# Group norms by two products with a tile of ones and the root on all partitions, and state renewals on more ticks, in a hybrid decoder step

## Chip, cores and metric

The kernel runs on one core of a Trainium2 chip. The metric is device time in microseconds (us) of one execution, as the median of several; smaller is better. The core has five engines that run their own instruction streams and meet by semaphores: TensorE (PE, its weight loads PEld), VectorE (DVE), ScalarE (ACT), GpSimd (POOL) and SyncE (SP, which here only issues DMAs).

## What is computed

One layer of a hybrid decoder for 256 new prompt tokens and 64 sample tokens (8 sequences of 8), so 320 tokens with a model width of 2048. One input projection feeds two groups of heads: a gated chunk MLP and a state-space mixer (SSD, Mamba-2). Their outputs go through `w_out`, then comes a feed-forward block with a short convolution. All values are float32. Cut to what the change touches:

```python
def rms_norm(x, w):
    y = x * rsqrt(mean(x * x, axis=-1, keepdims=True) + EPS)
    return y * w

def ssd_mixer(z, xbc, dt_raw, ssm_state, ...):
    ...                                   # convolution, silu, dt
    y, new_state = ssd_scan(xs, dt, a, bm, cm, ssm_state)
    y = (y + d_skip[:, None] * xs).reshape(bsz, L, SSM_WIDTH) * silu(z)
    # the group norm: 4 groups of 512 of the 2048 columns, each with its own mean square
    yg = y.reshape(bsz, L, SSM_GROUPS, SSM_WIDTH // SSM_GROUPS)
    yg = yg * rsqrt(mean(yg * yg, axis=-1, keepdims=True) + EPS)
    y = yg.reshape(bsz, L, SSM_WIDTH) * norm_w
    return y, new_state, new_conv

def decoder_layer(x, ...):
    h = rms_norm(x, norm_mix_pre)
    proj = h @ w_in
    mix = concatenate([gate_out, ssm_out]) @ w_out
    x = x + rms_norm(mix, norm_mix_post)
    f, new_ffn_conv = conv_ffn(rms_norm(x, norm_ffn_pre), ...)
    x = x + rms_norm(f, norm_ffn_post)
```

The states of the 8 sample sequences (each 32 heads x 64 x 128) are outputs too: the old state times its whole decay, plus a product of the 8 new tokens' columns B and of their decayed inputs.

## The kernel before

**Layout.** Activations lie transposed: 128 columns of the model on the partitions, the 320 tokens along the free dimension. A product with weights takes a block of 128x128 weights as the stationary operand and 320 tokens as the moving one.

**Products in parts.** Float32 is computed in three products of a rounded type (`F32R`): both operands are split in a high part, rounded to that type, and a low part, the rest. `accumulate` (L143 to L145) issues high weights by high input, high by low and low by high. `slab` fetches 128x1024 weights by a DMA on SP (tile `wraw`), makes the high part `whi` on ACT (L130) and the low part `wlo` on DVE (L132); each of the three has three buffers. `split` (L367) does the same for activations.

**Passes.** `project` runs one pass over 512 columns of a weight matrix (8 slabs of 24 products), `chunk_out` adds 512 rows of an output matrix into an accumulator (8 slabs of 24 products, evacuated by ACT or DVE, L234 and L236).

**Background tasks and ticks.** What is not a pass is written as generators in a list `bg`. After each slab a pass calls `tick()` `rate` times, and each call advances the first task in the list to its next `yield`; `repeat(None, n)` lets n ticks go by. So the tick decides after which slab a step is written down. Within each engine the instructions are then ordered by a scheduler at build time: by order of writing, unless `first()` or `high_priority` gives a block precedence, and never ahead of what it depends on. `issue_after(x)` keeps an instruction behind x on its engine. What stands in that order is executed in that order.

**The group norm.** `heads_out(g, rate, later)` is called for the four groups g. Its pass makes z; for each block of 128 columns it multiplies y by silu(z), squares it on ACT and adds the squares into `ssq` on DVE (L302), so `ssq` holds for each token 128 partial sums, one a partition. Then the task `norm` is put at the head of `bg`, to run during the next passes: after `later[0]` ticks `token_sums` (L284) lets PE sum `ssq` over the partitions, as three products with a column of ones in float32, which gives the tokens' sums along the partitions (128x3); `rsqrt_of` (L245) takes the reciprocal root of these three columns on DVE, a first guess by integer arithmetic and three Newton steps, eleven operations with precedence; after `later[1]` more ticks `spread` (L288, products L292) brings the result to all partitions and 320 columns by three transposes on PE, and four multiplications (L960), each with a `split` by the norm's weight, make the input of the chunk of `w_out`. `later` is (3, 2) for all groups but the third, where it is (4, 3). The ticks a slab are 1 in the pass behind the first and second norm, 3 behind the third (the pass of the fourth group's z) and 2 behind the fourth (a chunk of `w_out`). `rsqrt_of` has one more user, the layer norm of the gate, on three columns.

**The renewals.** The task `renewals` runs in the feed-forward part, where each of ten rounds of an up-projection and a down-chunk has 24 ticks, and must be finished before the eleventh chunk. It ends three prompt states (`rest`, two ticks each), loads the decays and the first four sample states, then the tokens' columns (`tokens`, 16 DMAs on SP into `xb`). For each of four groups it lets 3 ticks go by, copies the columns (L1191, ACT), masks the low half (L1194, DVE), and for both halves multiplies four states by their decay on POOL (L1199, a tick each), loads the next states, waits two ticks, issues four products of 32 rows on PE (`up_ps`, L1211), adds them to the states on DVE (L1213, a tick each) and stores the states (L1215, from ACT).

**Buffers that matter.** The tag `pv` of the pool `tp` has four buffers of 128x320; the z passes use it for `ev`. PSUM is halved: four banks `mm` for passes and chunks, four banks `ms` (`misc`) for the rest.

Of the kernel before, what the change touches and what calls it, by code (L numbers as in the profile page):

```python
# [9 lines left out]
F32 = mybir.dt.float32  # L10
F32R = mybir.dt.float32r
# [6 lines left out]
P = 128  # L18
# [3 lines left out]
NT = NP + NS  # L22
# [12 lines left out]
def hybrid_step(  # L35
# [10 lines left out]
    act, dve, pool, pe, sp = nc.scalar, nc.vector, nc.gpsimd, nc.tensor, nc.sync  # L46
# [3 lines left out]
    cp = ctx.enter_context(tc.tile_pool(name="cp", bufs=1))  # L50
    dr = ctx.enter_context(tc.tile_pool(name="dr", bufs=1, space=DRAM))
    wp = ctx.enter_context(tc.tile_pool(name="wp", bufs=3))
    tp = ctx.enter_context(tc.tile_pool(name="tp", bufs=2))
# [3 lines left out]
    def misc(name):  # L57
        return ms.tile([P, 512], F32, tag="ms", name=name)
# [6 lines left out]
    with tc.high_priority(offset=300000):  # L65
        dve.memset(ones, 1.0)

        ps = misc("early")
        for _ in range(EARLY):
            pe.matmul(ps[:, :P], ones, ones, start=True, stop=True)  # L70
    upper = cp.tile([P, P], F32, name="upper")
    later = cp.tile([P, P], F32, name="later")
    bd2 = cp.tile([P, P], F32, name="bd2")
# [3 lines left out]
    bd = bd2[:NS, :NS]  # L77

    def masks():
        make_upper_triangular(nc, upper, 1.0, diag=True)  # L80
        make_lower_triangular(nc, later, 1.0, diag=False)
        pool.memset(bd2, 0.0)
        for op, fill, base in ((ALU.is_gt, 1.0, 1 - TS), (ALU.is_ge, 0.0, 0)):
            pool.affine_select(out=bd2, in_=bd2, pattern=[[-TS, P // TS], [0, TS]], compare_op=op, fill=fill, base=base,
                               channel_multiplier=1)

        d4 = ident.rearrange("p (i r t) -> p i r t", r=4, t=TS)
        dve.tensor_reduce(out=low[:, 0:1], in_=d4[:, :, 2:4], axis=mybir.AxisListType.XYZ, op=ALU.add)
        d5 = ident.rearrange("p (i k t) -> p i k t", k=2, t=TS)
        dve.tensor_reduce(out=low[:, 1:2], in_=d5[:, :, 1], axis=mybir.AxisListType.XY, op=ALU.add)  # L90
        dve.tensor_scalar(out=low, in0=low, scalar1=-1.0, scalar2=None, op0=ALU.mult)
        for r in range(2):
            rs = slice(64 * r, 64 * r + 64)
            dve.tensor_tensor(out=upper_s[rs], in0=upper[rs, rs], in1=bd2[rs, rs], op=ALU.mult)
        pool.memset(cmask, 1.0)
        cm4 = cmask.rearrange("p (h b) i -> p h b i", h=2)
        pool.affine_select(out=cm4, in_=cm4, pattern=[[0, 2], [-8, 4], [1, 32]],
                           compare_op=ALU.is_ge, fill=0.0, base=0, channel_multiplier=0)
        pool.affine_select(out=cm4, in_=cm4, pattern=[[0, 2], [8, 4], [-1, 32]],
                           compare_op=ALU.is_ge, fill=0.0, base=7, channel_multiplier=0)  # L100
# [8 lines left out]
    def first():  # L109

        return tc.high_priority(offset=200000)
# [130 lines left out]
        pd_last.append(made)  # L242


    def rsqrt_of(ss, scale, n, rows=P):  # L245

        v = tp.tile([P, n], F32, tag=f"rs_v{n}", name="rs_v")[:rows]
        r = tp.tile([P, n], F32, tag=f"rs_r{n}", name="rs_r", bufs=3)[:rows]
        t = tp.tile([P, n], F32, tag=f"rs_t{n}", name="rs_t")[:rows]
        dve.tensor_scalar(out=v, in0=ss, scalar1=scale, scalar2=EPS, op0=ALU.mult, op1=ALU.add)  # L250
        dve.tensor_scalar(out=r.bitcast(I32), in0=v.bitcast(I32), scalar1=-0.5, scalar2=float(0x5F3759DF),
                          op0=ALU.mult, op1=ALU.add)
        for _ in range(3):
            dve.scalar_tensor_tensor(out=t, in0=v, scalar=-0.5, in1=r, op0=ALU.mult, op1=ALU.mult)
            dve.tensor_tensor(out=t, in0=t, in1=r, op=ALU.mult)
            ins = dve.scalar_tensor_tensor(out=r, in0=t, scalar=1.5, in1=r, op0=ALU.add, op1=ALU.mult).ins
        rsqrt_ins.append(ins)
        return r
# [20 lines left out]
    def token_sums(sq, ps=None, more=False):  # L279

        begins = ps is None
        ps = misc("tsum") if begins else ps
        for c, o in enumerate((0, P, NT - P)):
            ins = pe.matmul(ps[:, c:c + 1], sq[:, o:o + P], ones[:, 0:1], start=begins and c == 0, stop=not more and c == 2).ins  # L284
        sums_ins.append(ins)
        return ps if more else ps[:, 0:3]

    def spread(r, out=None):  # L288

        ps = misc("spread")  # L290
        for c, o in ((2, NT - P), (0, 0), (1, P)):
            spread_ins.append(pe.transpose(ps[:, o:o + P], r[:, c:c + 1].to_broadcast([P, P]), ident).ins)  # L292
        if out is not None:
            act.copy(out, ps[:, :NT])
        return ps[:, :NT]
# [94 lines left out]
    with ExitStack() as mctx:  # L390
# [350 lines left out]
        with tc.tile_pool(name="sd", bufs=1) as sd:  # L741
# [6 lines left out]
            for c in range(3):  # L748
                ps = misc("bt_ps")
# [184 lines left out]
            def heads_out(g, rate, later):  # L934

                ssq = hp.tile([P, NT], F32, tag="ssq", name="ssq")
                y = x_of.pop(g)

                def z_evac(j, ps):
                    if j == 0:  # L940
                        finish(tasks[g])
                    zs = tp.tile([P, NT], F32, tag="ev", name="zs", bufs=2)
                    with first():
                        scaled(ps, AF.Silu, zs)
                        dve.tensor_tensor(out=y[:, j, :], in0=y[:, j, :], in1=zs, op=ALU.mult)
                        add_square(ssq, y[:, j, :], j == 0, dve)
                project(w_in, Z0 + 512 * g, z_evac, quiet=4, rate=rate)

                def norm():
                    yield from repeat(None, later[0])  # L950
                    with tc.issue_after(newest[0]):
                        sums = token_sums(ssq)
                    with first():
                        r = rsqrt_of(sums, 1.0 / 512, 3)
                    yield from repeat(None, later[1])
                    rb = spread(r)

                    res[g] += [h[:, KD - 4:] for h in hT] if g == 3 else out_parts(hp, "o")
                    for j in range(4):
                        dve.tensor_tensor(out=y[:, j, :], in0=y[:, j, :], in1=rb, op=ALU.mult)  # L960
                        split(res[g][0][:, j, :], res[g][1][:, j, :], y[:, j, :], col(prm_at["norm"][3] + 4 * g + j))
                task = norm()
                bg.insert(0, task)
                return task
# [98 lines left out]
    with tc.tile_pool(name="fp", bufs=1) as fp:  # L1063
# [91 lines left out]
        def renewals():  # L1155
# [4 lines left out]
            for g, s1, x1d, _ in rest:  # L1160
                yield from repeat(None, 2)
                with tc.issue_after(rsqrt_ins[-1]):
                    dve.tensor_tensor(out=s1, in0=s1, in1=x1d, op=ALU.add)
                act.dma_start(o_ssm_p[g], s1)

            def load(g, h):

# [19 lines left out]
                tokens(0)  # L1187
            for g in range(4):
                h0 = 8 * g
                yield from repeat(None, 3)  # L1190
                act.copy(part, raw)  # L1191
                yield
                for at, m in ((slice(0, 512), 0), (slice(512, 640), 1)):
                    dve.scalar_tensor_tensor(out=part[:, :, at], in0=part[:, :, at].bitcast(F32), scalar=low[:, m:m + 1], in1=raw[:, :, at],  # L1194
                                             op0=ALU.mult, op1=ALU.add)
                for h in range(2):
                    st = ahead.pop(0)
                    for i in range(4):
                        pool.tensor_tensor(out=by_head(st[i]), in0=by_head(st[i]),  # L1199
                                           in1=tote[:, h0:h0 + 8, 4 * h + i:4 * h + i + 1].to_broadcast([P, 8, 64]), op=ALU.mult)  # L1200
                        yield
                    if h == 0:
                        ahead.append(load(g, 1))
                    elif g < 3:
                        ahead.append(load(g + 1, 0))
                        tokens(g + 1)
                    yield from repeat(None, 2)
                    grown = [misc("up_ps") for _ in range(4)]
                    for i in range(4):
                        at = slice(32 * i, 32 * i + 32)  # L1210
                        pe.matmul(grown[i], part[at, h, 512:], part[at, h, :512], start=True, stop=True, tile_position=(32 * i, 0))  # L1211
                    for i in range(4):
                        dve.tensor_tensor(out=st[i], in0=st[i], in1=grown[i], op=ALU.add)  # L1213
                        yield
                        act.dma_start(o_ssm_s[4 * h + i, g], st[i])  # L1215
# [179 lines left out]
```

## Time and profile before

| | |
|---|---|
| median of 3 runs | 1760.93 us (1760.37 to 1761.53) |
| the profiled execution's own time | 1762.04 us |
| its span in the profile | 1760.3 us |
| busy: PE, PEld, DVE, ACT, POOL | 1751.6, 1729.8, 1154.1, 806.6, 272.7 us |
| instructions on PE | 12178 products and as many weight loads |
| granted PE clock | 0.999 of full speed |
| DMA | 301.38 MB, 171 GB/s in the mean |

The span is shorter than the execution's own time by what lies before its first and behind its last instruction. Rows of a timeline give start (us from the span's start), duration (us), engine, line, operation, tiles (out<-in), shapes and count; a bracket at the end gives the engine's idle time before it and what ended it. Rows of groups give count, then busy us and mean ns of one, then idle time before them and what ended it. A matmul's duration in the profile contains its way through the array, so what a product costs PE in a stream is read from the distance between starts. A float32 product on PE stands as two instructions.

### The profile page before, as it was taken

What the parts mean: (1) busy time and instruction counts of PE and PEld (TensorE: products, weight loads), DVE (VectorE), ACT (ScalarE), POOL (GpSimd) and SP (SyncE); (2) the same over time, 40 slices, a digit from 0 to 9 for tenths busy, and PEclk for the clock granted to TensorE, in tenths of its full rate; (3) what the DMA queues carried; (4) which work ended last, traced back from release to release, by engine and by line L of the source; (5) the groups of instructions that cost most, each with busy time, mean ns of one, the idle gap of its engine ahead of it and who ended that gap; (6) DMA issues with size and microseconds to landing.
All of it is one profiled execution on the core that took longest, in us unless ns stands there. A gap on an engine that the chain in (4) does not pass through costs nothing.

```text
span 1760.3 us, 31124 instructions
## 1 busy us (share of the span) xinstructions
PE 1751.6 (100%) x12178; PEld 1729.8 (98%) x12178; DVE 1154.1 (66%) x1949; ACT 806.6 (46%) x1172; POOL 272.7 (15%) x588
## 2 busy tenths in 40 slices
PE   9999999999999999999999999999999999999998
PEld 9999999999999999999999999999999999999997
DVE  7449754656767576668966677676657565656575
ACT  7344545333854445545544434343434343333335
POOL 1003200000111101021331212130201010111004
PEclk9999999999999999999999999999999999999999
DMA  7466655456665644554756666756454545454542
GB/s 248 144 167 182 185 151 150 153 155 190 216 206 163 201 145 131 166 161 143 228 169 223 189 217 195 222 185 192 151 153 148 156 148 155 148 155 147 155 151 104
DMA packets 228179, 301.38 MB, mean 171 GB/s; under 512 B 19936, under 2 KB 150848, under 8 KB 227840
## 3 DMA queue, kind: packets, MB, share of 16 engines
q1 hardware_dynamic: 215856, 281.27, 52.4%
q10 hardware_dynamic: 10640, 13.60, 2.2%
q0 software_dynamic: 1536, 4.52, 1.0%
q8 instruction: 96, 1.57, 0.4%
q14 instruction: 51, 0.42, 0.1%
HBM read 283.47 MB, written 15.61 MB: 170 GB/s over the span
## 4 chain that ended last, share of the span: by engine, by line
PE 95%; DVE 2%; DMA 1%; ACT 0%; POOL 0%; issue 0%; SPq 0%; POOLq 0%; DVEq 0%; ACTq 0%
PE ps L143 20%; PE ps L145 20%; PE ps L144 20%; PE pd L143 10%; PE pd L144 10%; PE pd L145 10%; PE y_ps L900 1%; DMA wraw<-in_ffn_w_up 1%; DVE wlo L132 1%; PE yo_ps L848 0%; PE sg L705 0%; PE tsum L284 0%; DVE h_lo L374 0%; DVE acc_mix L1042 0%; DMA vt<-in_xT 0%; ACT whi L130 0%
## 5 line engine op out<-in xcount | busy, mean ns | idle before, releaser
L132 DVE TENSOR_TENSOR wlo<-wraw,whi 128x1024 fp32r<-128x1024 f32 x470 | 582.9, 1241 | 436.9 <-ACT whi L130 434.9
L130 ACT CAST whi<-wraw 128x1024 fp32r<-128x1024 f32 x470 | 492.0, 1047 | 730.3 <-PE ps L144 437.7
L143 PE MATMUL ps<-h_hi,whi 128*128 128x320 f32 x2528 | 782.1, 310 | 0.4 <-ACT whi L130 0.4
L144 PE MATMUL ps<-h_lo,whi 128*128 128x320 f32 x2528 | 779.8, 309 | 0.0
L145 PE MATMUL ps<-h_hi,wlo 128*128 128x320 f32 x2528 | 777.8, 309 | 0.0
L143 PEld LDWEIGHTS ps<-h_hi,whi 128*128 128x128 f32 x2528 | 474.8, 188 | 4.2 <-issue 2.3
L144 PEld LDWEIGHTS ps<-h_lo,whi 128*128 128x128 f32 x2528 | 475.1, 188 | 0.0
L145 PEld LDWEIGHTS ps<-h_hi,wlo 128*128 128x128 f32 x2528 | 474.4, 188 | 0.1
L143 PE MATMUL pd<-fhi,whi 128*128 128x320 f32 x704 | 217.2, 309 | 0.0
L144 PE MATMUL pd<-flo,whi 128*128 128x320 f32 x704 | 217.0, 308 | 0.0
L145 PE MATMUL pd<-fhi,wlo 128*128 128x320 f32 x704 | 216.9, 308 | 0.0
L143 PE MATMUL pd<-ohi,whi 128*128 128x320 f32 x448 | 139.5, 312 | 0.0
L145 PE MATMUL pd<-ohi,wlo 128*128 128x320 f32 x448 | 138.5, 309 | 0.0
L144 PE MATMUL pd<-olo,whi 128*128 128x320 f32 x448 | 138.5, 309 | 0.0
L143 PEld LDWEIGHTS pd<-fhi,whi 128*128 128x128 f32 x704 | 132.2, 188 | 0.7 <-issue 0.7
L144 PEld LDWEIGHTS pd<-flo,whi 128*128 128x128 f32 x704 | 132.2, 188 | 0.2 <-issue 0.2
L145 PEld LDWEIGHTS pd<-fhi,wlo 128*128 128x128 f32 x704 | 132.2, 188 | 0.0
L1099 POOL COPY ptf<-pad 128x2 f32<-128x2 f32 x88 | 24.2, 275 | 508.3 <-DVE pad L1087 507.5
L236 DVE TENSOR_TENSOR acc_ffn<-acc_ffn,pd 128x320 f32<-128x320 f32 x160 | 77.2, 482 | 34.5 <-PE pd L145 33.6
L143 PEld LDWEIGHTS pd<-ohi,whi 128*128 128x128 f32 x448 | 84.0, 188 | 1.4 <-issue 0.7
L144 PEld LDWEIGHTS pd<-olo,whi 128*128 128x128 f32 x448 | 84.1, 188 | 0.2 <-issue 0.2
L145 PEld LDWEIGHTS pd<-ohi,wlo 128*128 128x128 f32 x448 | 84.1, 188 | 0.0
(301 smaller groups left out, 1513.6 us busy)
## 6 DMA issues: line engine op xcount, KB each, us to landing
wraw<-in_ffn_w_up SPq DMA_DIRECT2D x176, 512.0 KB
wraw<-in_w_in SPq DMA_DIRECT2D x142, 512.0 KB
wraw<-in_ffn_w_down SPq DMA_DIRECT2D x88, 512.0 KB
wraw<-in_w_out SPq DMA_DIRECT2D x64, 512.0 KB
st<-in_state_ssm SPq DMA_DIRECT2D x64, 256.0 KB
out_ssm_state_sample<-st ACTq DMA_DIRECT2D x32, 256.0 KB
cs<-dacs_d SPq DMA_DIRECT2D x16, 320.0 KB
xr<-in_xT SPq DMA_DIRECT2D x4, 640.0 KB
```

The costliest lines, as they stand in the source:

```text
L130: act.copy(hi[:, :m], raw[:, :m])
L132: dve.tensor_tensor(out=lo[:, :m], in0=raw[:, :m], in1=hi[:, :m].bitcast(F32), op=ALU.subtract)
L143: pe.matmul(ps, whi, xhi, start=first, stop=False)
L144: pe.matmul(ps, whi, xlo, start=False, stop=False)
L145: newest[0] = pe.matmul(ps, wlo, xhi, start=False, stop=last).ins
L236: dve.tensor_tensor(out=acc[:, nb, :], in0=acc[:, nb, :], in1=ps[:, :NT], op=ALU.add)
L900: pe.matmul(ps[64 * i:64 * i + 64, cols], w(hl), x(hl, m, cpx), tile_position=(0, 64 * i), **flags)
L1099: pool.tensor_copy(ptf[:, k, :], pad[:, 256:258])
```

## The change

Four edits. (1) A second tile of ones in the rounded type, `ones_r`, is made from `ones` by a copy on DVE among the masks. (2) In `norm`, the squares are split into a high and a low part (ACT and DVE, with precedence), two ticks sooner than the sums were asked for; one tick behind that, two products of `ones_r` (128x128) with the parts (128x320) give the sums of all tokens on all partitions. The eleven operations of the root then run on 128x320, with `rb` and two buffers of `pv` for its places, and there are no transposes: the four multiplications read `rb`. They are written at the same tick as before, since `later[1] + 1` ticks follow. (3) `rsqrt_of` takes its places from the caller if given. (4) In `renewals`, four ticks follow the prompt states, the first group lets 12 ticks go by in place of 3, and each multiplication on POOL takes two ticks in place of one.

```diff
     def masks():
+        dve.tensor_copy(ones_r, ones)
         make_upper_triangular(nc, upper, 1.0, diag=True)
...
-    def rsqrt_of(ss, scale, n, rows=P):
+    def rsqrt_of(ss, scale, n, rows=P, places=None):
 
-        v = tp.tile([P, n], F32, tag=f"rs_v{n}", name="rs_v")[:rows]
-        r = tp.tile([P, n], F32, tag=f"rs_r{n}", name="rs_r", bufs=3)[:rows]
-        t = tp.tile([P, n], F32, tag=f"rs_t{n}", name="rs_t")[:rows]
+        v, r, t = places or (tp.tile([P, n], F32, tag=f"rs_{name}{n}", name=f"rs_{name}", bufs=bufs)[:rows]
+                             for name, bufs in (("v", 2), ("r", 3), ("t", 2)))
...
                 def norm():
-                    yield from repeat(None, later[0])
+                    yield from repeat(None, later[0] - 2)
+                    parts = [tp.tile([P, NT], F32R, tag="pv", name="ssq_part", bufs=4) for i in range(2)]
+                    with first():
+                        split(*parts, ssq)
+                    yield
+                    ps = misc("tsum")
                     with tc.issue_after(newest[0]):
-                        sums = token_sums(ssq)
+                        for i in range(2):
+                            pe.matmul(ps[:, :NT], ones_r, parts[i], start=i == 0, stop=i == 1)
                     with first():
-                        r = rsqrt_of(sums, 1.0 / 512, 3)
-                    yield from repeat(None, later[1])
-                    rb = spread(r)
+                        rb = sd.tile([P, NT], F32, tag="rb", name="rb", bufs=1)
+                        v, t = (tp.tile([P, NT], F32, tag="pv", name=f"rs_{n}", bufs=4) for n in "vt")
+                        rsqrt_of(ps[:, :NT], 1.0 / 512, NT, places=(v, rb, t))
+                    yield from repeat(None, later[1] + 1)
...
                 act.dma_start(o_ssm_p[g], s1)
+            yield from repeat(None, 4)
...
             for g in range(4):
                 h0 = 8 * g
-                yield from repeat(None, 3)
+                yield from repeat(None, 3 if g else 12)
                 act.copy(part, raw)
...
                                            in1=tote[:, h0:h0 + 8, 4 * h + i:4 * h + i + 1].to_broadcast([P, 8, 64]), op=ALU.mult)
+                        yield
                         yield
```

More of the change, by code (lines that the diff above doesn't have):

```diff
@@ L70, in hybrid_step @@
             pe.matmul(ps[:, :P], ones, ones, start=True, stop=True)
+    ones_r = cp.tile([P, P], F32R, name="ones_r")
     upper = cp.tile([P, P], F32, name="upper")
```

## Prediction

> **What bounds the kernel now.** I read the page first: busy times, then the chain that ended last.
>
> ```profile
> span 1760.3 us, 31124 instructions
> ...
> PE 1751.6 (100%) x12178; PEld 1729.8 (98%) x12178; DVE 1154.1 (66%) x1949; ACT 806.6 (46%) x1172; POOL 272.7 (15%) x588
> ...
> PE 95%; DVE 2%; DMA 1%; ACT 0%; POOL 0%; issue 0%; SPq 0%; POOLq 0%; DVEq 0%; ACTq 0%
> ```
>
> TensorE (PE) is busy all the time and is 95% of the chain; VectorE (DVE) has a third of the span free. A busy PE need not be at its peak, so I looked next at the distances between matmuls, in the timeline of PE around the first group norm:
>
> ```profile
> 529.83 0.31 PE L144 MATMUL ps<-h_lo,whi 128*128 128x320 f32 x1
> ...
> 536.57 0.31 PE L145 MATMUL ps<-h_hi,wlo 128*128 128x320 f32 x1
> 536.72 0.72 PE L284 MATMUL tsum<-ones,ssq 128*128 128x1 f32 x6
> 537.30 0.39 PE L143 MATMUL ps<-h_hi,whi 128*128 128x320 f32 x1
> 537.53 0.31 PE L144 MATMUL ps<-h_lo,whi 128*128 128x320 f32 x1
> ...
> 544.28 0.31 PE L145 MATMUL ps<-h_hi,wlo 128*128 128x320 f32 x1
> 544.42 0.49 PE L292 MATMUL spread<-ident,rs_r 128*128 128x128 f32 x3
> 544.67 0.40 PE L143 MATMUL ps<-h_hi,whi 128*128 128x320 f32 x1
> 544.90 0.31 PE L144 MATMUL ps<-h_lo,whi 128*128 128x320 f32 x1
> ```
>
> The first two rows are 46 steps and 6.74 us apart: one product every 147 ns, without a hole. So time can be won in one way only: issue less on PE, or remove one of its rare waits. Work on other engines is free until PE waits for it. 0.2% of the time, 3.5 us, is about what a measurement of this kernel can tell from no change; the question is whether the change takes more than that off PE.
>
> **The norms: what goes.** From the product before the sums to the second one behind them it is 537.53 - 536.57 = 0.96 us, where two steps take 0.29: the sums cost 0.67. The transposes cost 544.90 - 544.28 - 0.29 = 0.33. I measure to the second product because the first one behind an f32 product holds up the next (537.30 to 537.53 is 0.23, not 0.15). A norm costs 1.00 us of PE, and the tile view counts four of them, six sum products each; in the last one PE also waited before its transposes:
>
> ```profile
> L284 PE MATMUL tsum<-ones,ssq x24: 165/250/250, 536.7 to 751.0; 128*128 128x1 f32 x24
> ...
> 755.32 0.31 PE L144 MATMUL pd<-olo,whi 128*128 128x320 f32 x1
> 755.64 0.51 PE L292 MATMUL spread<-ident,rs_r 128*128 128x128 f32 x3
> ...
> 756.14 0.30 PE L143 MATMUL pd<-ohi,whi 128*128 128x320 f32 x1
> ```
>
> 756.14 - 755.32 - 0.29 = 0.53, so 0.20 more than elsewhere. Removed in all: 4 x 1.00 + 0.20 = 4.2 us.
>
> **The norms: what comes.** Two products of 128x320 with both operands in the rounded type, as the main products have, so at their 147 ns, without the late product behind: 4 x 2 x 0.147 = 1.2 us. The trace has no product with this weight tile; the bounds are 0.29 (the main step) and 0.67 (the sums now) a norm, and I take the first, since shape and type are the main product's. By the Trainium skill, page "TensorE: Matmul & The Clock Gate", section "Back-to-back issue gap", an isolated gap is N/2.4 + 2.5 ns, 136 ns for 320 columns; here the trace shows 147, and by the page's figure the sum would be lower by 0.1 us.
>
> **The norms: what moves to the other engines.** The two parts of the squares cost a copy on ScalarE (ACT) and a subtraction on DVE per norm, and the root runs on 320 columns instead of 3: the same eleven operations. The groups by line give the price of one:
>
> ```profile
> L302 DVE TENSOR_TENSOR ssq<-ssq,sq 128x320 f32<-128x320 f32 x12 | 5.8, 486 | 1.9 <-ACT sq L301 1.8
> L371 DVE TENSOR_TENSOR olo<-s,ohi 128x320 fp32r<-128x320 f32 x16 | 7.7, 484 | 0.6 <-ACT ohi L370 0.5
> L255 DVE TENSOR_TENSOR rs_t<-rs_t,rs_r 128x3 f32<-128x3 f32 x15 | 2.4, 160 | 0.4
> ```
>
> 0.49 us each where it was 0.16. The narrow root's place in DVE's timeline, with what lies around it:
>
> ```profile
> 526.44 0.49 DVE L302 TENSOR_TENSOR ssq<-ssq,sq 128x320 f32<-128x320 f32 x1 [0.60 <-ACT sq L301]
> ...
> 537.48 0.16 DVE L250 TENSOR_SCALAR rs_v<-tsum 128x3 f32<-128x3 f32 x1 [1.88 <-PE tsum L284]
> 537.67 0.17 DVE L251 TENSOR_SCALAR rs_r<-rs_v 128x3 int32<-128x3 int32 x1
> ...
> 538.35 1.22 DVE L132 TENSOR_TENSOR wlo<-wraw,whi 128x1024 fp32r<-128x1024 f32 x1
> ...
> 540.47 0.16 DVE L256 SCALAR_TENSOR_TENSOR rs_r<-rs_t,rs_r 128x3 f32<-128x3 f32 x1
> ...
> 544.95 0.89 DVE L960 TENSOR_TENSOR xs<-xs,spread 128x320 f32<-128x320 f32 x2 [1.68 <-PE spread L292]
> ```
>
> Operations start 0.16 + 0.03 us apart (537.48 to 537.67), so the wide chain takes about 11 x 0.52 = 5.7 us instead of 2.1. The squares are final at 526.9. The parts are asked for two ticks sooner than the sums are now and the products one tick sooner, at the first and second norm about 533 instead of 536.7 (a tick is a slab, 24 steps or 3.5 us). The chain then ends near 534 + 5.7 + 1.2 for one slab's subtraction inside it = 541, and the four multiplications by the root, at 544.95 now because they wait for the transposes, can start 3 to 4 us sooner. At the third and fourth norm, where more ticks fall on a slab, the products stay in their place and the multiplications come some 3 us later than now. In these rows of DVE and PE stand their first (third norm), the first product that uses them, their last (fourth norm) and again the first product:
>
> ```profile
> 726.10 0.88 DVE L960 TENSOR_TENSOR xs<-xs,spread 128x320 f32<-128x320 f32 x2 [0.80 <-PE spread L292]
> 743.50 0.31 PE L143 MATMUL pd<-ohi,whi 128*128 128x320 f32 x1
> 762.24 0.48 DVE L960 TENSOR_TENSOR xs<-xs,spread 128x320 f32<-128x320 f32 x1
> 772.86 0.31 PE L143 MATMUL pd<-h_hi,whi 128*128 128x320 f32 x1
> ```
>
> 17 and 10 us of room; 3 us later costs nothing. What hides the added 3.6 + 0.5 us of DVE per norm is its idle time:
>
> ```profile
> 525.00:553.00 28.00, 28.00 (x195) 27.99 (x195) 16.99 (x38) 11.50 (x15) 1.56 (x6) 1.00 0.50 154
> ```
>
> (PE, PEld, DVE, ACT, POOL, clock.) 28 - 17 = 11 us are free. Queued behind the chain on DVE are the subtractions that make a slab's low part. How late may one be?
>
> ```profile
> 536.77 1.05 ACT L130 CAST whi<-wraw 128x1024 fp32r<-128x1024 f32 x1 [2.43 <-PE ps L144]
> ```
>
> ACT rounds a slab as soon as PE frees one of three buffers, two slabs before the product that needs it: 7.0 - 1.05 - 1.22 = 4.7 us of cover. A chain cut up by subtractions, as now at 538.35, stays inside it; cost nothing. If the cover is gone, each us over it is a us of PE.
>
> Without the transposes the multiplications no longer come late for the output chunks of the first two norms. The weight loads of these chunks waited for them:
>
> ```profile
> L143 PEld LDWEIGHTS pd<-ohi,whi 128*128 128x128 f32 x448 | 84.0, 188 | 1.4 <-issue 0.7 <-ACT s L832 0.4 <-ACT ohi L373 0.3
> ```
>
> 0.3 us for ACT's part of the result. I count it as won (bounds 0 and 0.3).
>
> The cast of ones, on DVE, is ready to run as soon as ones is set, and DVE is idle there:
>
> ```profile
> 0.91 0.17 DVE L66 MEMSET ones<- 128x128 f32 x1 [0.91 <-PEq L1386]
> 3.81 0.55 DVE L578 SCALAR_TENSOR_TENSOR h_lo<-vt,h_hi 128x320 fp32r<-128x320 f32 x1 [2.74 <-ACT h_hi L577]
> ```
>
> It costs nothing there, and at most its own 0.2 us if it is put into the full stretch behind; I take nothing.
>
> **The renewals.** Eight groups of four products go to PE. One group made it wait, as the groups by line and the timeline show:
>
> ```profile
> L1211 PE MATMUL up_ps<-xb_parts 32*128 32x512 f32 x32 | 4.0, 494 | 0.6 <-DVE xb_parts L1194 0.6
> ...
> 932.01 0.40 SPq L1180 DMA_DIRECT2D xb<-xb_d  x1
> ...
> 938.08 2.48 DVE L1194 SCALAR_TENSOR_TENSOR xb_parts<-xb_parts,low,xb 128x1024 fp32r<-128x1024 f32 x2 [0.26 <-DMA wraw<-in_ffn_w_up]
> ...
> 940.71 0.50 PE L1211 MATMUL up_ps<-xb_parts 32*128 32x512 f32 x4 [0.59 <-DVE xb_parts L1194]
> ```
>
> The last token load of the first group is issued at 932.0, the parts are done at 940.6, and PE stood 0.6 us for them. The change asks for the loads 4 ticks later (14 us), for the copy 13 ticks later and for the products 17 ticks later (60 us): the loads are long there, so I count 0.6 us as won (bounds 0 and 0.6). The other seven groups show no wait; their turn grows from 24 to 32 ticks, so the loads of states through SP and the stores through ACT have more time, not less. The renewals take 45 ticks more, about 150 in all; the ten rounds before the one that must finish them give 240, so nothing is left for the end.
>
> **The sum.** -4.2 + 1.2 - 0.3 - 0.6 = -3.9 us. The profiled execution took 1762.04 us, 1.7 outside its span of 1760.3, and lies 1.1 over the median of the runs; from the median the sum gives 1760.9 - 3.9 = 1757.0 us, which is 0.22% faster: just over the bound.
>
> **The rivals.** *The waits stay or others come.* The order on every engine is laid out anew, and the new products can wait for the parts of the third norm, or the renewals meet other work in their new places, where till now they stood at the same tick of every round. If the 0.3 and 0.6 stay, it is 1757.9; with another 1 to 2 us of waits, 1758 to 1760: within 0.2%. For it: PE's rare waits come from just such places. Against it: with DVE more than half busy PE hardly ever waited. *The change does not do what it says for PE:* a product with the ones costs as much as the sums now. Then 4 x 0.67 = 2.7 comes back instead of 1.2: 1758.5. Little speaks for it.
>
> *The wide root shuts out the slabs.* It has precedence over the subtractions, so it may run as a block before one. A block of 5.7 us is 1.0 over the cover of 4.7, four times: the gain is eaten up, 1761. It gets worse if GpSimd (POOL) works beside it, as these rows of DVE and POOL show:
>
> ```profile
> 883.38 5.97 DVE L132 TENSOR_TENSOR wlo<-wraw,whi 128x1024 fp32r<-128x1024 f32 x3 [0.19 <-ACT whi L130]
> ...
> 883.21 5.06 POOL L1199 TENSOR_TENSOR st<-st,tote 128x512 f32<-128x512 f32 x3
> ```
>
> 2.0 us an operation against 1.22 alone, a factor of 1.6. With it the block takes 9.3 us, PE waits 4.6 four times, and the time is 1757.0 + 18 = 1775. It decides, as slower by 0.2%, from (3.9 + 3.5) / 4 = 1.9 us over the cover, a block of 6.6 us, 0.60 an operation. Against it: POOL is busy for 1.56 of the 28 us around the norm, and a subtraction did slip into the narrow chain. By the Trainium skill, page "SBUF — State Buffer", section "Who interferes with whom", a DVE instruction with two SBUF inputs contends with a GpSimd instruction that reads SBUF; the trace agrees, with 2.0 against 1.22. Nine of the eleven operations are of that kind.
>
> **How the numbers follow.** The sum as it stands, 1756.3 to 1757.4: 0.52. Waits that stay or come, or dear products, 1757.4 to 1760.5: 0.33. The root as a block that eats the gain, around 1761: 0.06. Slower by the block with contention, or by renewals that hold up PE by as much: 0.09. So faster 0.52, same 0.39, slower 0.09. The range leaves out 0.1 on the slow side and some on the other: 1756.2 to 1760.6.
>
> **What would show it.** In the timeline of PE the step across a norm's two products is 0.29 us more than the plain one, and the six sum products and three transposes of each norm are gone; on DVE the root's operations last 0.49 us and are cut by subtractions of slabs; PE has no idle time before up_ps. A hole in PE before a product with wlo, within 10 us of a norm, would show the block. A span shorter by more than 4.2 us would mean that I missed a wait; one shorter by less than 3 us, that a norm's products cost more than 0.29 us or that new waits came, and the idle time by line tells which.

## The result and the profile after

The changed kernel takes 1764.52 us, median of 11 executions (1762.18 to 1766.79), against 1761.30 (1760.37 to 1761.53) for the kernel before: a ratio of 1.0019 (95% interval 1.0010 to 1.0028). It is slower by 3.2 us, where 3.9 us less were forecast. The profiled execution took 1765.49 us. The page of the changed kernel says where to look:

```profile
span 1763.8 us, 31062 instructions
...
PE 1751.6 (99%) x12150; PEld 1729.0 (98%) x12150; DVE 1162.7 (66%) x1954; ACT 810.3 (46%) x1176; POOL 273.7 (16%) x588
```

PE has 28 instructions fewer and the same busy time, in a span 3.5 us longer: some of its work has become slower, and PE now waits.

**The norms did what was forecast.** The timeline of PE around the first norm of the changed kernel (start, us, engine and line, operation):

```profile
532.73 0.31 PE L146 MATMUL ps<-h_lo,whi 128*128 128x320 f32 x1
532.87 0.31 PE L147 MATMUL ps<-h_hi,wlo 128*128 128x320 f32 x1
533.02 0.46 PE L959 MATMUL tsum<-ssq_part,ones_r 128*128 128x320 f32 x2
533.31 0.31 PE L145 MATMUL ps<-h_hi,whi 128*128 128x320 f32 x1
```

533.31 - 532.87 = 0.44 us, a plain step and 0.29 us for the two products. There is no late product behind them. The gain can be read further on, where PE reaches the first unread product of the mixing norm; in the kernel before and in the changed one:

```profile
801.02 0.46 PE L1001 MATMUL unread<-h_hi 128*128 128x320 f32 x2
```

```profile
797.52 0.45 PE L1009 MATMUL unread<-h_hi 128*128 128x320 f32 x2
```

PE is 3.5 us ahead there; 0.2 us of it it already had in front of the first norm, from the start of the program, so the norms themselves gave 3.3. And the wait before the states' products is gone, by the groups by line:

```profile
L1221 PE MATMUL up_ps<-xb_parts 32*128 32x512 f32 x32 | 4.0, 495 | 0.0
```

**Then the gain was lost in two places.** Busy time by stretch (PE, PEld, DVE, ACT, POOL; then PE's granted clock, DMA share, GB/s), changed kernel first, then the kernel before at the same work:

```profile
845.00:848.00 3.00, 1.53 (x13) 1.29 (x12) 2.03 (x3) 1.26 (x2) 0.00 (x0) 1.00 0.44 115
848.00:851.50 3.50, 3.50 (x15) 3.50 (x15) 3.07 (x8) 0.20 (x1) 0.00 (x0) 0.53 0.62 173
...
894.00:902.00 8.00, 7.80 (x54) 7.57 (x53) 7.05 (x9) 1.66 (x3) 8.00 (x9) 1.00 0.36 114
902.00:906.50 4.50, 1.65 (x10) 1.13 (x8) 1.20 (x1) 2.28 (x4) 2.25 (x12) 0.97 0.03 7
906.50:909.60 3.10, 3.02 (x11) 3.02 (x12) 2.39 (x3) 1.42 (x2) 0.00 (x0) 0.50 0.55 181
```

```profile
849.00:853.00 4.00, 3.30 (x25) 3.06 (x24) 2.91 (x9) 1.25 (x2) 0.00 (x0) 1.00 0.44 131
898.00:906.00 8.00, 8.00 (x57) 8.00 (x56) 3.79 (x4) 2.81 (x4) 1.04 (x2) 1.00 0.68 206
906.00:910.00 4.00, 4.00 (x29) 4.00 (x28) 1.36 (x2) 1.05 (x1) 0.00 (x0) 1.00 0.44 141
```

Look at the products in a stretch in which PE is full: 15 in 3.50 us and 11 in 3.02 where the clock stands near 0.5, against 29 in 4.00 before. In the timeline of PE the products of these stretches follow each other after 0.27 us instead of 0.147. The trace's record of the clock has two such stretches, of 3.413 us each; the kernel before has none between its start and its end. The number of stretches differs from execution to execution: the mean granted clock of the eleven lies between 1.000 (the shortest, 1762.18 us) and 0.996 (the longest, 1766.79 us), and one stretch takes 0.001 off it.

**The second place, 894 to 910 us, step by step.** The load of the decays (`tote`) on SP, before and after:

```profile
871.39 0.50 SPq L1183 DMA_DIRECT2D tote<-tote_d  x1
```

```profile
884.23 0.46 SPq L1192 DMA_DIRECT2D tote<-tote_d  x1
```

Four ticks, 12.8 us later. POOL of the kernel before and of the changed one:

```profile
876.22 6.63 POOL L1199 TENSOR_TENSOR st<-st,tote 128x512 f32<-128x512 f32 x5 [0.77 <-DMA tote<-tote_d]
```

```profile
888.04 1.07 POOL L1208 TENSOR_TENSOR st<-st,tote 128x512 f32<-128x512 f32 x1 [11.13 <-DMA tote<-tote_d]
889.05 0.48 POOL L1106 COPY stg<-pad 128x16 f32<-128x16 f32 x1
...
889.61 5.64 POOL L1208 TENSOR_TENSOR st<-st,tote 128x512 f32<-128x512 f32 x4
...
896.10 4.62 POOL L1208 TENSOR_TENSOR st<-st,tote 128x512 f32<-128x512 f32 x3
...
901.23 1.06 POOL L1208 TENSOR_TENSOR st<-st,tote 128x512 f32<-128x512 f32 x1
...
902.42 1.06 POOL L1208 TENSOR_TENSOR st<-st,tote 128x512 f32<-128x512 f32 x1
...
903.54 0.19 POOL L1106 COPY stg<-pad 128x16 f32<-128x16 f32 x1
```

Before, the first eight multiplications stood in a pause of POOL between two evacuations. Now ten of them, the eight and two more, wait 11 us for the decays and stand in POOL's order among the copies of the convolution's last columns (`stg`, L1106; written by the up-projection of the second group), the last of which ends at 903.7. ACT of the changed kernel:

```profile
895.65 0.49 ACT L1109 ACTIVATE gcv<-gcv 128x336 f32<-128x336 f32 x1
903.77 0.34 ACTq L1151 DMA_DIRECT2D out_ffn_conv_sample<-stg  x1
904.22 1.04 ACT L132 CAST whi<-wraw 128x1024 fp32r<-128x1024 f32 x1 [8.09 <-POOL pad L1092]
```

ACT has nothing to compute for 8 us: next in its order is the store of `stg`, and behind it the rounding of a slab that PE needs. (The bracket names POOL's instruction right behind the last copy, a memset at 903.68; that the store is what holds ACT up is tested below.) What PE saw:

```profile
902.78 0.31 PE L147 MATMUL ps<-h_hi,wlo 128*128 128x320 f32 x1
905.32 0.42 PE L145 MATMUL ps<-h_hi,whi 128*128 128x320 f32 x1 [2.23 <-ACT whi L132]
905.58 0.31 PE L146 MATMUL ps<-h_lo,whi 128*128 128x320 f32 x1
906.58 0.64 PE L147 MATMUL ps<-h_hi,wlo 128*128 128x320 f32 x1 [0.70 <-DVE wlo L134]
907.01 0.47 PE L145 MATMUL ps<-h_hi,whi 128*128 128x320 f32 x1
907.28 0.47 PE L146 MATMUL ps<-h_lo,whi 128*128 128x320 f32 x1
```

905.32 - 902.78 - 0.15 and 906.58 - 905.58 - 0.15 are 3.2 us of waits. With a smaller one at 894.4 and the slow products behind, PE loses 5.3 us here: the same product is 1.24 us ahead of the kernel before at 894 us and 4.03 us behind it at 912.

**The first place, 845 to 851 us**, is the sums of the norm ahead of the feed-forward part, before and after:

```profile
850.01 0.69 PE L284 MATMUL tsum<-ones,sq 128*128 128x1 f32 x5 [0.70 <-DVE sq L302]
```

```profile
847.24 0.80 PE L285 MATMUL tsum<-ones,sq 128*128 128x1 f32 x6 [1.47 <-DVE sq L303]
```

The wait is 0.77 us longer, and 13 products behind it at half clock cost 0.12 us more each, 1.6 us. The balance: -3.5 + 0.8 + 1.6 + 5.3 - 0.6 (the states' products) = +3.6 us, against 3.5 us between the spans.

### The profile page after: what moved, and what is told of

It is laid out like the page before. It is cut to its first block, busy times and chain, and to the rows that moved or that the text cites. A ratio compares the mean times of both kernels' runs of the same rounds, so it can differ in the third digit from the quotient of the medians.

```text
span 1763.8 us, 31062 instructions
## 1 busy us (share of the span) xinstructions
PE 1751.6 (99%) x12150; PEld 1729.0 (98%) x12150; DVE 1162.7 (66%) x1954; ACT 810.3 (46%) x1176; POOL 273.7 (16%) x588
## 3 DMA queue, kind: packets, MB, share of 16 engines
q8 instruction: 96, 1.57, 0.4%
## 4 chain that ended last, share of the span: by engine, by line
PE 97%; DVE 1%; POOL 1%; issue 0%; ACT 0%; DMA 0%; SPq 0%; POOLq 0%; ACTq 0%; DVEq 0%
PE ps L145 21%; PE ps L147 21%; PE ps L146 20%; PE pd L145 10%; PE pd L147 10%; PE pd L146 10%; PE y_ps L901 1%; DVE wlo L134 0%; PE yo_ps L849 0%; PE sg L706 0%; PE vt_ps L591 0%; POOL st L1208 0%; DMA vf<-in_w_in 0%; PE tsum L285 0%; POOL acc_ffn L1281 0%
```

## The experiments

The theory after the traces (theory 1): the four ticks behind the prompt states let the decays come late, POOL's multiplications then stand in front of copies that ACT's store waits for, and the weights' rounding waits behind the store. Rivals: the wide root and the split of the squares cost the time (2); the longer spreads do, or the later loads on the queues (3). Theory 4 concerns the first place: the longer wait there brings PE to half clock, in some executions.

**Each half alone.** The kernel before with the norms' edits only, and with the renewals' edits only (the diff shown above, cut in two).

> The kernel before with the two-product norms alone; the states' renewals stay where they were. Theory 1 (the four extra ticks behind the rest cause the loss, the norms gain what was forecast): near 1757.5 us, 3.4 us under the kernel before, no row of the first group's whi waiting 8 us before an ACT CAST near 904 us, PE's granted clock without a stretch at half between 890 and 915 us. Rival 2 (the norms' wide root and split cost the time somewhere behind the norms): 1763 to 1765 us, as with the whole change. Rival 3 (the longer spreads of the renewals cost the time): 1757.5 us as well. The wait of 0.66 us before the first states' projection (940 us) should still be there by theory 1, so 1757.0 to 1758.0.

> The kernel before with the three edits of the renewals alone (double steps, four ticks behind the rest, twelve ticks in the first group); norms as before. Theory 1: 1761.3 plus 5 to 8 us less 0.6 us, that is 1766 to 1768 us; the wide state's load issued about 13 us later, the first multiplications of POOL in front of the copies of the convolution's state, ACT's rounding of the weights waiting about 8 us near 907 us, and PE at half clock behind it. Rival 2 (the norms cost the time): 1760.5 to 1761 us, no such wait.

The norms alone: 1758.65 us (1757.96 to 1760.21), ratio 0.9988 (0.9979 to 0.9997). The renewals alone: 1766.53 (1764.73 to 1767.70), ratio 1.0028 (1.0017 to 1.0038), that is +5.2 us. The latter's profile has the whole chain without any new norm; its POOL and its ACT:

```profile
890.68 5.64 POOL L1200 TENSOR_TENSOR st<-st,tote 128x512 f32<-128x512 f32 x4
```

```profile
905.28 1.04 ACT L130 CAST whi<-wraw 128x1024 fp32r<-128x1024 f32 x1 [8.08 <-POOL pad L1084]
```

In that execution of the renewals alone PE waits for the slab as in the changed kernel (2.21 and 0.70 us, at 906 and 907), but its clock stays at 1.00: the half clock that was expected is not there. Its time is 1765.28 us. The three executions with a mean clock of 1.000 took 1764.7 to 1765.3 us, the five at 0.999 and less 1766.4 to 1767.7. So the renewals' move costs 3.4 to 4.0 us without half clock, and half clock comes on top in some executions.

Rival 2 falls. The norms alone came 0.7 us above the place expected: six of their executions lie at 1758.0 to 1758.7, five at 1760.0 to 1760.2; that is taken up below.

**The four ticks.** The changed kernel without them, and the new norms with them as the only edit of the renewals:

```diff
                 act.dma_start(o_ssm_p[g], s1)
-            yield from repeat(None, 4)
```

> The changed kernel without the four ticks behind the rest; the double steps and the twelve ticks of the first group stay. Theory 1: 1756.8 to 1757.5 us, POOL's first multiplications of the state end before 890 us as in the kernel before, no half clock near 906 us. Rival 3 (the longer spreads, not the four ticks, cost the time): 1763 to 1765 us. Rival 2 (the norms): 1763 to 1765 us too.

> The norms of the changed kernel and, of the renewals, the four ticks behind the rest alone; single steps and three ticks as before. Theory 1: 1763.5 to 1766 us, with the wait of ACT's rounding near 904 us and half clock behind it. Rival 3 (the longer spreads cost the time): 1757 to 1758 us.

Without: 1758.59 us (1757.49 to 1760.20), ratio 0.9986 (0.9977 to 0.9994), which is 1.1 us above the place expected. With them alone: 1764.27 (1763.25 to 1766.77), 1.0018 (1.0010 to 1.0027), and ACT's rounding waits 8.09 us at 902.2. So this one line carries the loss, and the other edits of the renewals cost nothing that can be measured. POOL of the kernel without the ticks is back in its pause:

```profile
873.23 6.80 POOL L1207 TENSOR_TENSOR st<-st,tote 128x512 f32<-128x512 f32 x5 [1.06 <-DMA tote<-tote_d]
...
881.13 5.07 POOL L1207 TENSOR_TENSOR st<-st,tote 128x512 f32<-128x512 f32 x3
```

**Which link: late loads, POOL's order, or ACT's store?** All with the four ticks and the late loads. First POOL's order: each multiplication of the first group is kept behind the copy that was written last before it.

```diff
-                pool.tensor_copy(ptf[:, k, :], pad[:, 256:258])
+                copied.append(pool.tensor_copy(ptf[:, k, :], pad[:, 256:258]).ins)
...
-                        pool.tensor_tensor(out=by_head(st[i]), ...
+                        with nullcontext() if g else tc.issue_after(copied[-1]):
+                            pool.tensor_tensor(out=by_head(st[i]), ...
```

> The changed kernel with its four ticks and its late loads; only POOL's order differs: each multiplication of the first group comes behind the copy of the convolution's last columns that was written before it in the program, so two instead of eight multiplications stand in front of the second group's copies. Theory 1 (the order on POOL is the cause): 1757.5 to 1759.5 us, no rounding that waits 8 us near 904 us. Rival 3 (the later loads of the states themselves, on the DMA queues, cost the time): 1763 to 1765 us as with the whole change.

1758.25 us (1757.46 to 1760.00), ratio 0.9985 (0.9976 to 0.9994). The decays still come 11.3 us late for POOL, and PE is full (columns as above):

```profile
894.00:902.00 8.00, 8.00 (x56) 8.00 (x56) 4.13 (x6) 3.20 (x5) 1.44 (x4) 1.00 0.66 204
902.00:906.50 4.50, 4.50 (x33) 4.50 (x32) 1.76 (x2) 1.05 (x1) 0.00 (x0) 1.00 0.40 134
```

So the late loads by themselves cost nothing; it is the order. Then ACT's store, moved to POOL, in a first try for the wrong group:

```diff
-                act.dma_start(o_fconv_s[:, k:k + 4], stg[:, half])
+                (act if g else pool).dma_start(o_fconv_s[:, k:k + 4], stg[:, half])
```

> The changed kernel; only the two stores of the first group's convolution state of each kind (stg) are issued by POOL instead of ACT, so that no store stands in ACT's order in front of the weights' rounding. The order of POOL's multiplications and copies stays as in the changed kernel. Theory 1 (POOL's copies late, ACT's store waits for them, the rounding behind the store): the 8.1 us wait of ACT's rounding near 904 us is gone, the gaps of PE at 902 to 910 us (5 us together in the changed kernel's profile) with it: 1758.5 to 1760 us. If instead the late multiplications hurt by sharing the memory with DVE, or by the pads that POOL clears late: 1762 to 1765 us, with PE waiting near 903 us for something else than ACT's rounding behind a store.

1764.69 us (1762.59 to 1767.41): nothing gained. Its ACT shows why: the store in question is the second group's and still there.

```profile
904.27 0.34 ACTq L1151 DMA_DIRECT2D out_ffn_conv_sample<-stg  x1
904.73 1.04 ACT L132 CAST whi<-wraw 128x1024 fp32r<-128x1024 f32 x1 [9.10 <-POOL pad L1093]
```

With `(pool if g == 1 else act)` in that line:

> The changed kernel; the two stores of stg of the second group are issued by POOL instead of ACT. (The copies that come late near 900 us are the second group's, which runs one step ahead; the run with the first group's stores moved did not touch the store in question.) POOL's order of multiplications and copies stays. Theory 1 with ACT's store as the link: the 8.1 us wait of ACT's rounding near 904 us is gone and 3.4 us of PE's gaps at 902 to 907 us with it, the half clock behind them too: 1758.5 to 1760.5 us. If the link is another (the pads that POOL clears late, DVE sharing the memory with POOL): 1762 to 1765 us.

1760.82 us (1758.55 to 1761.46), ratio 0.9993 (0.9985 to 1.0002), 0.3 us above the place expected: 3.7 us of the changed kernel's time are gone with ACT's store. POOL's order is unchanged and its copies are as late (the last one ends at 904.1), but ACT rounds on time and PE is full; the timeline of ACT, then the stretches:

```profile
898.94 1.03 ACT L132 CAST whi<-wraw 128x1024 fp32r<-128x1024 f32 x1
```

```profile
894.00:902.00 8.00, 8.00 (x57) 8.00 (x56) 7.61 (x7) 3.47 (x5) 8.00 (x9) 1.00 0.36 103
902.00:906.50 4.50, 4.50 (x32) 4.50 (x32) 2.17 (x2) 1.05 (x1) 4.09 (x10) 1.00 0.94 269
```

DVE is busy for 7.61 of the 8 us where the kernel with the copies first needs 4.13. The same three operations on DVE, here beside POOL's multiplications and with the copies first:

```profile
894.58 3.94 DVE L1104 SCALAR_TENSOR_TENSOR gcv<-pad,prm,gcv 128x336 f32<-128x336 f32 x3
```

```profile
893.47 1.64 DVE L1106 SCALAR_TENSOR_TENSOR gcv<-pad,prm,gcv 128x336 f32<-128x336 f32 x3
```

3.94 us instead of 1.64. In this part PE waits once, for 0.4 us at 892, for DVE's evacuation of a bank (L1096).

**The wait at the sums (theory 4).** Executions of the kernels without the loss lie in two groups, 1.8 to 1.9 us apart in the mean: 5 of 11, 5 of 11 and 3 of 11 at 1759.8 to 1760.2 for the norms alone, without the ticks and with the copies first. Seven products that nobody reads were put behind the sums:

```diff
+                made = sums_ins[-1]
+                for i in range(7):
+                    with first(), tc.issue_after(made):
+                        made = pe.matmul(ps[:, :NT], hT[0][:, i, :P], hT[0][:, i, :], start=True, stop=True).ins
```

> The changed kernel without the four ticks, and with seven products that nobody reads behind the sums of the norm ahead of the feed-forward part (near 846 us), 7 x 147 ns = 1.03 us of work in a wait of 0.9 to 1.7 us. Theory 4 (the executions at 1760 us of the kernels without the four ticks are those in which this wait brings PE to half clock for 3.4 us, 13 products x 0.12 us = 1.6 us): all executions within 1757.3 to 1758.8 us, median near 1758.0. Rival (the products only take room, the two groups of times come from elsewhere): two groups of times as before, or both 0.1 to 1 us higher.

> The whole change, with POOL's multiplications of the first group behind the copies and with the seven unread products behind the sums near 846 us. Theories 1 and 4 together: 1757.5 to 1759 us with all executions in one group; without theory 4 two groups 1.7 us apart; without theory 1 1762 to 1765 us.

They missed: 1759.40 us (1758.51 to 1761.90) and 1759.13 (1758.74 to 1759.36), 0.8 and 0.9 us up, since PE waits ahead of the sums, not behind them. The first still has two groups; the second has one, and why is not shown. Then six such products ahead of the sums:

```diff
+                ps_other = mm.tile([P, 512], F32, tag="mm", name="ps_other")
+                made = newest[0]
+                for i in range(6):
+                    with first(), tc.issue_after(made):
+                        made = pe.matmul(ps_other[:, :NT], hT[0][:, i, :P], hT[0][:, i, :], start=True, stop=True).ins
                 ps = misc("ps_one")
...
-                ps = mm.tile([P, 512], F32, tag="mm", name="ps_other")
+                ps = ps_other
```

> The changed kernel without the four ticks, and with six products that nobody reads between the last product before the sums of the norm ahead of the feed-forward part and these sums, where the trace shows PE idle for 0.9 to 1.5 us behind DVE's squares: 6 x 147 ns = 0.88 us. (The seven products of the run before stood behind the sums, where PE did not wait, and cost their 1.03 us.) Theory 4 (PE at half clock after this wait in some executions makes the second group of times): median 1757.8 to 1758.4 us, all executions within 1757.3 to 1759.0, none near 1760. Rival (the second group comes from elsewhere): two groups again, 1.7 us apart.

> The whole change with POOL's multiplications of the first group behind the copies, and the six unread products ahead of the sums near 846 us. Theories 1 and 4: median 1757.5 to 1758.3 us, one group of times. Rival to theory 4: two groups, 1.7 us apart, as in the run with the copies first alone.

> The whole change with the second group's two stores of stg issued by POOL, and the six unread products ahead of the sums near 846 us. Moving the stores alone gave 1760.8 us in the middle, 1758.6 in the execution with the profile. If what is left above 1758.3 us comes from the wait at the sums near 846 us (half clock behind it): 1757.8 to 1758.6 us. If it comes from the second group's stretch (DVE slowed by POOL's multiplications between 888 and 904 us, a short wait of PE there and half clock behind that): 1760 to 1761 us still.

Without the ticks: 1758.14 us (1757.81 to 1759.42), ratio 0.9983 (0.9974 to 0.9992), the shortest time of all. With the copies first: 1758.29 (1757.57 to 1760.24), 0.9984 (0.9976 to 0.9993). With the second group's store on POOL: 1759.45 (1758.95 to 1759.91), 1.4 us less than without the filling, and between the two places expected. Each kernel's executions now form one group, but for the 1760.24 us (and, between the two former groups, 1759.42 without the ticks and 1759.14 with the copies first). The 1760.24 us happens to be the execution with the profile, and there the half clock can be seen:

```profile
847.36 0.80 PE L285 MATMUL tsum<-ones,sq 128*128 128x1 f32 x6 [1.14 <-DVE sq L303]
```

```profile
848.00:851.50 3.50, 3.50 (x17) 3.46 (x17) 2.28 (x8) 0.20 (x1) 0.00 (x0) 0.61 0.80 222
```

In that execution DVE's squares came late enough for a wait of 1.14 us in spite of the filling. In the profile without ticks and with the filling, PE did not wait for the sums at all, and its clock stayed at 1.00. The profiles of the norms alone, without the ticks and with the copies first are of executions of the lower groups (1758.17, 1758.20, 1757.74) and have no half clock either: theory 4 holds as far as the traces reach. The other executions have no profile, but their mean granted clock is on record. In these three kernels it is 0.9997 in the mean of the 20 executions of the lower groups and 0.9987 in the mean of the 13 of the upper ones; the difference, 0.001, is one stretch of 3.413 us at half clock. With the store moved and no filling, the seven executions from 1760.45 us up have 0.998 and the other four 0.999 or 1.000; with the filling, no execution of the three kernels is below 0.999.

> The same kernel as in the run with the second group's stores on POOL, for a profile of another execution. If it is one near 1760.8 us, its trace should show one or two stretches at half clock of 3.4 us: near 848 us by theory 4, near 895 to 905 us if DVE's slowing by POOL's multiplications makes PE wait there.

1759.05 us, in between, so this did not answer: no half clock, a wait of 1.18 us at the sums and one of 0.45 at 892. About 1.3 us between this kernel filled (1759.45) and the one without ticks filled (1758.14) stays open beyond that wait at 892. In the two profiles the span goes on for 4.5 and for 3.4 us behind POOL's last operation; whether these 1.1 us are chance is not shown.

**Why the wait at the sums varies.** In 14 of the 15 profiles the sums start 10.1 us behind the rounding of one certain slab on ACT (10.6 us with the renewals alone): the last squares stand behind it. That rounding waits for a transfer of weights. The same slab, the 218th of the program, before and after:

```profile
839.90 1.05 ACT L130 CAST whi<-wraw 128x1024 fp32r<-128x1024 f32 x1 [0.99 <-DMA wraw<-in_ffn_w_up]
```

```profile
837.13 1.05 ACT L132 CAST whi<-wraw 128x1024 fp32r<-128x1024 f32 x1 [2.50 <-DMA wraw<-in_ffn_w_up]
```

SP issued the transfer 3.5 us sooner than before (at 831.63 instead of 835.15), by as much as PE was ahead, but the rounding could start only 2.8 us sooner. The rest is the 0.8 us by which the wait grew. In the other profiles with the new norms and without the filling this rounding starts between 836.0 and 837.0 us, and the wait is between 0.70 and 1.57 us, longer in the main where the rounding is later. That a later landing makes the wait longer is read from the traces; no run moved the transfer alone.

## Why the prediction was wrong

- **Right: the norms' terms.** 0.29 us a norm for the products, no transposes, no waits of ACT's part: 3.3 us gained at 797 us (3.5 less the 0.2 from the start of the program), where -4.2 + 1.2 - 0.3 = -3.3 stood in the sum. The wide root's operations took 0.49 us and its chain at the first norm ended at 541.1, as expected, and no slab waited for them; that rival did not occur.
- **Right but small: the 0.6 us at the first states' products.** The wait is gone in every profile with moved renewals. In the time it does not show: 1758.59 us without the four ticks against 1758.65 for the norms alone.
- **Wrong: the renewals' move at nothing.** The step that failed is "the loads of states through SP and the stores through ACT have more time, not less". I followed the tokens' loads and the products on PE to their new places, and not the decays' load, POOL's multiplications and what they would then stand in front of. On POOL these are the copies of the second group, and who waits for a copy is a store in ACT's order. The row of 883.21 us that I quoted for the contention had these multiplications in it, in a pause that ended at 889.75 us. A term of 0 was +5.2 us by the run with the renewals alone. Its rival ("the renewals meet other work in their new places") named the kind of loss, with 1 to 2 us; the loss was 5. That renewals might make the kernel slower stood in the chances, with part of 0.09, but without a place or a mechanism.
- **Missing: the clock.** A wait was priced by its length. After a wait of 1.5 us, 13 products cost 1.6 us more. By the Trainium skill, page "TensorE: Matmul & The Clock Gate", section "What's actually happening", PE falls to half clock after an idle window of about 3.4 us, and the window runs freely. The traces agree with the length (3.413 us), the factor (0.27 us a step for 0.147) and the free run: within a trace the changes of the clock lie whole multiples of 3.413 us apart (843.092 us are 247 of them, 54.613 are 16, 853.332 are 250). They do not agree with a whole idle window: 1.14 us of wait within one was enough in one execution, 1.18 was not in another. Cut along this grid, with the sums' products of one column not counted as work, the 15 traces sort cleanly. Of the windows at full clock between 8 and 1740 us, the six in which PE was without work for 1.80 us or more are the six with half clock behind them; in all others it was 1.75 us or less. With the renewals alone the grid cuts the wait for the slab in two, 1.42 and 1.49 us, and the clock stays. So it seems to be the idle share of a window that decides, and where the grid lies differs between executions; this was found after the fact, and no run tested it.
- **What would show it** was half useful: the three signs that I named for the norms and for `up_ps` all came out right, and none of them looked at POOL or ACT between 870 and 910 us.

## What to carry to other kernels

When a background step is moved, list every instruction that it issues, on every engine, and for each the instructions that now stand behind it there, down to a DMA issue on a compute engine: in an engine's order a store that waits for a slow copy holds up everything behind it. A time at which an engine is idle is a resource that the old place may have used: POOL's pause at 876 to 889 us hid 11.7 us of work at no cost to PE. And work taken off the bounding engine lets it arrive sooner where transfers set the pace, so part of the gain can come back as a wait further on.

## What was not expected of the hardware

PE's granted clock fell to half for 3.413 us after single waits of only 1.14 us (copies first, filled), 1.47 us (the changed kernel) and 1.57 us (the first group's store on POOL), so a wait of that size can cost more than twice its length, and not in each execution. DVE beside POOL's multiplications took 3.94 us for three operations that take 1.64 alone, a factor of 2.4; the prediction used 1.6, from another operation (the slabs' subtractions).
